# A written order of steps between the first feed-forward and the input projections, with the first half's norm and first operand listed earlier

## The chip, the cores and the metric

The kernel runs on one core of one Trainium2 chip. The metric is the device time in microseconds (us) of one execution; lower is better. Times are compared by the median of several executions. TensorE does the matrix products (PE in the profile, and PEld for its weight loads), VectorE is DVE, ScalarE is ACT, GpSimd is POOL, and SyncE (SP) issues most transfers.

## The reference, cut to what matters

One layer works on 512 new prompt tokens and 64 sample tokens (8 sequences of 8), 576 columns in all, with a model width of 1024.

```
h = modulate(rms_norm(x, n1_g), sh1, sc1)
x = x + 0.5 * g1 * swiglu(h, w1_gate, w1_up, w1_down)     # FF = 2816
h = modulate(rms_norm(x, nm_g), sh2, sc2)
z = h @ w_in                                              # 10240 columns: u v q k rv rg ga gb
...                                                       # gMLP, retention, merge, second FFN
```

The change lies between the second and the fourth of these lines: the last products with `w1_down`, the sum into `x`, the norm of the new `x`, its shift and scale, and the first products with `w_in`. `modulate(n, shift, scale)` is `n * (1 + scale) + shift`; the norm is `x * rsqrt(mean(x*x) + EPS)` over the 1024 channels of a token.

## The kernel before, in words

Channels lie on the partitions: `x` is one tile of 128 partitions x 8 chunks x 576 tokens, called `x_90` in the orders below and `x` in the profile. Every product is made from three fp32r products of a high and a low part (`hi` is a rounded copy, `lo` is the value less `hi`), so each operand and each weight needs a copy on ScalarE (`hi`, lines 564, 566, 667, 669) and a subtraction on VectorE (`lo`, lines 571, 575, 675, 679). The products with `w_in` are made by a Strassen-like scheme on halves of the tokens (two halves of 288) and halves of the channels: the blocks of the operand are called N11 (channels 0 to 511, tokens of half 0, negated), B21 (channels 512 to 1023, half 0), N1, B22 and so on. Each block is a tile of 4 chunks x 288 tokens, made in two pieces of two chunks.

Around the change the order of the work is written out by hand, as a string of step names (`INTO_MIX`). The function `run` (line 198) issues the steps in that order and then ties the instructions of each engine, SyncE excepted, into that order. So each engine works off its own part of the string, first in first out, and waits at its head. SyncE's queue holds only loads; each waits for its buffer to come free. The step names:

- `Dch`: a product of the last group of the first feed-forward, output chunk c, token part h (18 matmuls, line 485). The two parts are the columns 0 to 319 and 320 to 575, not the halves of 288.
- `rsch`: adds it into `x` (VectorE, line 466; for h = 1 also line 471 for the sample tokens), and `pxc`: adds the sample tokens' part on GpSimd (line 472).
- `sqch`: the square of half h of chunk c (ScalarE, line 428); `adch`: adds the squares up (GpSimd, line 433; the last of a half on VectorE). `spch`: stores that half to memory through ScalarE's queue (line 1223).
- `rdh`: one product with ones that sums over the channels (PE, line 444); `rqh`: the reciprocal root (ScalarE, line 448); `q0h q1h q2h`: its refinement (VectorE, lines 456, 459, 461; `q2h` also stores the row from GpSimd's queue, line 1231).
- `xph`: multiplies two chunks (pair p) of half h by the norm, in place (VectorE, line 533, waits until the stores of these chunks have read them); `bpc0`, `bpc`: scale and shift of one chunk (ScalarE, line 540); `sp` with one digit: the same for the sample tokens (VectorE, line 549).
- `N11hj`, `N11lj`, `B21hj`, `B21lj`, ...: high and low part of a piece of a block.
- `nhi nli whi wli`: high and low parts of the two weight tiles of projection i (i = 0, 1). `h0ai` is its product with N11 (24 matmuls, line 651), `sni` copies the two banks out (ScalarE, line 660), `h0bi` is the product with B21 into the same banks, after `sni` has read them.

In the string before, after the last chunk of token half 0 (`D70 rs70 sq70 ad70`), the second projection's weights (`nh1 nl1 wh1 wl1`) and the products `D31`, `D41` and `D51` are listed around `rd0 rq0 q00 q10 q20`, all four scalings `x00 x10 x20 x30` are listed with the operand's pieces, and four of them run back to back on VectorE.

Of the kernel before, what the change touches and what calls it, by code (L numbers as in the profile page):

```python
# [54 lines left out]
D00 D01 rs00 Wh2 sp00 sq00 ad00 Wl2 D10 rs01 px0 Wh3 sq01 ad01 Wl3 D11 sp01 rs10 sp10 sq10  # L55
ad10 Wh6 D20 rs11 Wl6 px1 sq11 sp11 ad11 D21 Wh4 rs20 sq20 Wl4 sp20 ad20 D30 rs21 Wh5 px2
sq21 Wl5 sp21 ad21 D40 rs30 sq30 sp30 ad30 Wh7 Wl7 D50 rs40 sq40 sp40 nh0 ad40 D60 rs50
sq50 nl0 sp50 ad50 wh0 D70 rs60 sq60 sp60 wl0 ad60 D31 rs70 sq70 nh1 sp70 ad70 nl1 D41 rs31
px3 sq31 sp31 rd0 wh1 D51 ad31 rq0 rs41 px4 q00 sq41 wl1 q10 sp41 ad41 q20 D61 rs51 px5 x00 sq51
sp51 ad51 D71 x10 b000 b010 x20 b100 x30 b110 N11h0 rs71 N11h1 rs61 px7 b210 N11l0 px6  # L60
sq71 N11l1 sq61 sp61 sp71 b300 ad61 h0a0 b310 b200 ad71 B21h3 B21h2 B21l3 B21l2 rd1 sn0 h0a1
rq1 q01 q11 q21 x01 h0b0 x11 b01 b00 s0 b11 s1 b10 tx0 sn1 tx1 N1h0 x21 h0b1 N1h1 N1l0 N1l1
b20 x31 b21 T2a1 b31 b30 h1a0 s3 e0s1 s2 B22h3 N3c1 B22h2 T2b1 N3h1 B22l2 p2bh T2h1 B22l3
h1a1 p2ah p2bl T2l1 e0s0 e0m0 p2al e0m1 N3l1 h1b0 p2S N4c1 p2U N4h1 T2a0 p2Sh P1 e1t0 T2b0
e1m0 p2Sl T2h0 h1b1 e1a0 T2l0 e1s0 P1s p2V N3c0 p2Uh P2 N4c0 N3h0 p2Ul N4h0 P5 e1a1 N3l0
# [1989 lines left out]
```

## Time and profile before

| | before |
|---|---|
| time, median of 3 runs | 1652.28 us (1651.71 to 1655.64) |
| time of the profiled execution | 1651.52 us |
| its span in the profile | 1649.7 us |
| granted TensorE clock, mean of the span | 0.996 |
| PE busy | 1618.0 us (98%), 12548 matmuls |
| DVE busy | 1152.9 us (70%) |
| ACT busy | 783.2 us (47%) |
| POOL busy | 292.0 us (18%) |

Times in the timeline count from the start of the span, so the profiled execution has 1.8 us outside it. In a timeline row stand the start, the time from the start of its first to the end of its last instruction, the engine, the line, what it writes from what it reads, how often, and in brackets the idle time before it with what ended that. A row of the table by stretches has the stretch, its length, then busy time and number of instructions of PE, PEld, DVE, ACT and POOL, the granted clock, and the transfers' share and rate.

### The profile page before, as it was taken

How to read it: one execution, taken by the hardware profiler on the slowest of the kernel's cores; microseconds unless marked ns; L12 is line 12 of the kernel's file. 1: busy time of each engine (PE TensorE's matmuls, PEld its weight loads, DVE VectorE, ACT ScalarE, POOL GpSimd, SP SyncE). 2: the span in 40 equal slices, each digit the busy share in tenths (PEclk: the TensorE clock that was granted, in tenths of full speed). 3: DMA queues.
4: the chain of work that ended last, by engine and by line, in shares of the span. 5: the costliest groups of instructions: out<-in, count | busy, mean ns of one | idle time of the engine just before them, and what ended most of it. 6: DMA issues, size and time to landing. Idle time of an engine off the chain costs nothing. (4 is left out here: it accounts for less than half of the span.)

```text
span 1649.7 us, 31367 instructions
## 1 busy us (share of the span) xinstructions
PE 1618.0 (98%) x12548; PEld 1554.7 (94%) x12548; DVE 1152.9 (70%) x1835; ACT 783.2 (47%) x1331; POOL 292.0 (18%) x372
## 2 busy tenths in 40 slices
PE   7999999999999999999999999999999999999997
PEld 4899999999999999999999999998999999999997
DVE  6867856676697777854788554676848868676773
ACT  5644524344564556553444454443236525343454
POOL 0000000000411111113346343454231000000002
PEclk9999999999999999999999999999999999999999
DMA  9553444332536776765467575799540333332331
GB/s 292 152 157 110 141 129 139 110 110 84 183 115 212 228 214 192 222 196 187 126 192 248 180 172 159 208 261 270 177 141 14 87 93 97 91 96 80 100 90 58
DMA packets 300212, 252.09 MB, mean 153 GB/s; under 512 B 13593, under 2 KB 260633, under 8 KB 300066
## 3 DMA queue, kind: packets, MB, share of 16 engines
q1 hardware_dynamic: 284594, 206.76, 41.5%
q0 software_dynamic: 13168, 40.97, 8.8%
q10 hardware_dynamic: 2304, 2.36, 0.4%
q8 instruction: 98, 1.61, 0.4%
q14 instruction: 48, 0.39, 0.1%
HBM read 207.01 MB, written 43.02 MB: 152 GB/s over the span
## 5 line engine op out<-in xcount | busy, mean ns | idle before, releaser
L651 PE MATMUL ps<-xa,whl 128*128 128x288 f32 x3000 | 420.6, 295 | 5.8 <-ACT xa L564 2.4
L651 PEld LDWEIGHTS ps<-xa,whl 128*128 128x128 f32 x3000 | 401.7, 189 | 18.5 <-issue 5.0
L651 PE MATMUL ps<-xs,whl 128*128 128x288 f32 x2040 | 287.2, 294 | 1.3 <-ACT sn L660 1.1
L651 PEld LDWEIGHTS ps<-xs,whl 128*128 128x128 f32 x2040 | 272.2, 188 | 11.6 <-ACT sn L660 4.6
L679 DVE TENSOR_TENSOR whl<-wraw,whl 128x1024 fp32r<-128x1024 f32 x192 | 234.5, 1223 | 54.0 <-ACT whl L669 45.1
L669 ACT CAST whl<-wraw 128x1024 fp32r<-128x1024 f32 x192 | 200.2, 1048 | 107.0 <-DVE wraw L793 67.3
L485 PEld LDWEIGHTS ps<-c,wd 128*128 128x128 f32 x1824 | 236.7, 188 | 3.5 <-issue 3.4
L485 PE MATMUL ps<-c,wd 128*128 128x320 f32 (+1 forms) x1824 | 239.9, 292 | 0.0
L485 PE MATMUL ps<-c,whl 128*128 128x256 f32 (+1 forms) x1368 | 186.9, 294 | 1.1 <-ACT c L195 0.7
L485 PEld LDWEIGHTS ps<-c,whl 128*128 128x128 f32 x1368 | 179.4, 188 | 3.4 <-ACT c L195 1.2
L472 POOL TENSOR_TENSOR x<-x,s 128x64 f32<-128x64 f32 x72 | 35.2, 489 | 796.9 <-DVE s L471 771.0
L466 DVE SCALAR_TENSOR_TENSOR x<-ps,gate,x 128x320 f32<-128x320 f32 (+1 forms) x128 | 61.1, 481 | 110.7 <-PE ps L485 110.7
L660 ACT COPY sn<-ps 128x288 f32<-128x288 f32 x195 | 77.2, 398 | 104.0 <-PE ps L651 103.7
L188 DVE TENSOR_TENSOR whl<-wraw,whl 128x1024 fp32r<-128x1024 f32 x56 | 76.3, 1364 | 66.7 <-ACT whl L187 66.1
L952 ACT CAST wd<-wraw 128x640 fp32r<-128x640 f32 (+2 forms) x58 | 45.4, 783 | 102.6 <-PE ps L485 95.5
L1353 PE MATMUL ps<-whl,xx 128*128 128x256 f32 x768 | 88.9, 276 | 0.0
L1353 PEld LDWEIGHTS ps<-whl,xx 128*128 128x128 f32 x768 | 88.0, 188 | 0.0
L651 PE MATMUL ps<-xs,whs 128*128 128x288 f32 x480 | 69.1, 292 | 0.0
L187 ACT CAST whl<-wraw 128x1024 fp32r<-128x1024 f32 x56 | 58.6, 1049 | 21.5 <-PE ps L485 13.3
L669 ACT CAST whs<-wraw 128x512 fp32r<-128x512 f32 x62 | 38.4, 620 | 55.7 <-PE ps L651 45.0
L651 PEld LDWEIGHTS ps<-xs,whs 128*128 128x128 f32 x480 | 64.8, 188 | 0.0
L957 DVE TENSOR_TENSOR wd<-wraw,wd 128x640 fp32r<-128x640 f32 (+2 forms) x58 | 53.5, 922 | 10.6 <-ACT wd L952 10.5
(285 smaller groups left out, 2219.0 us busy)
## 6 DMA issues: line engine op xcount, KB each, us to landing
ada<-in_w_ada_dram SPq DMA_DIRECT2D x56, 512.0 KB
wraw<-in_w_in_dram SPq DMA_DIRECT2D x96, 256.0 KB
wraw<-in_w_gate_dram SPq DMA_DIRECT2D x88, 256.0 KB
wraw<-in_w_up_dram SPq DMA_DIRECT2D x88, 256.0 KB
wraw<-in_w_in_dram SPq DMA_DIRECT2D x32, 512.0 KB
wraw<-in_w_down_dram SPq DMA_DIRECT2D x32, 384.0 KB
wraw<-in_w_down_dram SPq DMA_DIRECT2D x32, 320.0 KB
accd<-c POOLq DMA_DIRECT2D x32, 288.0 KB, 5.9
```

Source lines behind the costliest of these rows:

```text
L187: ACT.copy(out=hi, in_=raw)
L188: now["lo"] = (eng or DVE).tensor_tensor(out=lo, in0=raw, in1=hi.bitcast(F32), op=ALU.subtract)
L466: DVE.scalar_tensor_tensor(out=x[:, o:o + w], in0=ps[:, :w], scalar=g[:, c, 0:1], in1=x[:, o:o + w], op0=ALU.mult, op1=ALU.add)
L472: return lambda: POOL.tensor_tensor(out=x[:, NP:T], in0=x[:, NP:T], in1=u, op=ALU.add)
L485: PE.matmul(ps[:, :PW[h]], lhsT=s[:, k, c0:c0 + P], rhs=m[:, PART[h]], start=k == 0 and z == 0, stop=k == kc - 1 and z == 2,)
L651: PE.matmul(ps[:, :H], lhsT=s[:, j * P:(j + 1) * P], rhs=m[:, j, :], start=fresh and j == 0 and z == 0, stop=j == 3 and z == 2, skip_group ...
L660: ACT.copy(out=t, in_=ps[:, :H])
L669: ACT.copy(out=hl[:, 0], in_=src)
L679: now["lo"] = DVE.tensor_tensor(out=hl[:, 1], in0=src, in1=hl[:, 0].bitcast(F32), op=ALU.subtract)
L952: ACT.copy(out=hl[:, 0], in_=self.raw[c])
L957: DVE.tensor_tensor(out=lo, in0=self.raw[c], in1=hi.bitcast(F32), op=ALU.subtract)
L1353: PE.matmul(ps[:, :DV], lhsT=s, rhs=m, start=i == 0, stop=i == 23)
```

## The change

The change rewrites three lines of the string `INTO_MIX` and leaves all functions, sizes, buffers and step names as they are.

```diff
 sq21 Wl5 sp21 ad21 D40 rs30 sq30 sp30 ad30 Wh7 Wl7 D50 rs40 sq40 sp40 nh0 ad40 D60 rs50
-sq50 nl0 sp50 ad50 wh0 D70 rs60 sq60 sp60 wl0 ad60 D31 rs70 sq70 nh1 sp70 ad70 nl1 D41 rs31
-px3 sq31 sp31 rd0 wh1 D51 ad31 rq0 rs41 px4 q00 sq41 wl1 q10 sp41 ad41 q20 D61 rs51 px5 x00 sq51
-sp51 ad51 D71 x10 b000 b010 x20 b100 x30 b110 N11h0 rs71 N11h1 rs61 px7 b210 N11l0 px6
-sq71 N11l1 sq61 sp61 sp71 b300 ad61 h0a0 b310 b200 ad71 B21h3 B21h2 B21l3 B21l2 rd1 sn0 h0a1
-rq1 q01 q11 q21 x01 h0b0 x11 b01 b00 s0 b11 s1 b10 tx0 sn1 tx1 N1h0 x21 h0b1 N1h1 N1l0 N1l1
+sq50 nl0 sp50 ad50 wh0 D70 rs60 sq60 sp60 wl0 ad60 D31 rs70 sq70 sp70 ad70 nh1 rd0 rs31 D41
+px3 rq0 sq31 sp31 q00 wh1 ad31 q10 q20 rs41 px4 x00 sq41 sp41 ad41 D51 b000 x10 b010 rs51 px5
+N11h0 nl1 b100 b110 N11l0 D61 N11h1 sq51 sp51 rs61 px6 N11l1 ad51 sq61 sp61 D71 rs71 px7 ad61
+x20 sq71 sp71 h0a0 b200 b210 x30 B21h2 ad71 wl1 rd1 rq1 b300 b310 B21h3 q01 sn0 h0a1 q11 q21
+B21l2 B21l3 x01 h0b0 x11 b01 b00 s0 b11 s1 b10 tx0 sn1 tx1 N1h0 x21 h0b1 N1h1 N1l0 N1l1
```

On PE, `rd0` moves ahead of `D41` (it stood behind it), and `D71` moves behind `D61` as before; nothing else of PE's order changes. On VectorE the place from the last residual of half 0 to the operand's first low part reads, before (`ps_4871` is the bank of `rd0`, `h_4895` the norm, `whl_4840` and `whl_4873` the second projection's weights, `gate` the gate of the feed-forward):

```order
L675 SCALAR_TENSOR_TENSOR whl_4840<-wraw_4565,whl_4840 128x1024
L466 SCALAR_TENSOR_TENSOR x_90<-ps_4818,gate_1251,x_90 128x192
L456 SCALAR_TENSOR_TENSOR h_4901<-h_4895 128x288
L679 TENSOR_TENSOR whl_4873<-wraw_4568,whl_4873 128x1024
L459 SCALAR_TENSOR_TENSOR h_4901<-ps_4871,h_4901 128x288
L461 SCALAR_TENSOR_TENSOR h_4895<-h_4901,h_4895 128x288
L533 TENSOR_TENSOR x_90<-x_90,h_4895 128x2x288 x4
L571 SCALAR_TENSOR_TENSOR xa_4965<-x_90,xa_4965 128x2x288 x2
```

The same place of the changed kernel (`ps_4844`, `h_4869`, `whl_4842`, `whl_4876` and `xa_4917` are the same tiles under new numbers):

```order
L466 SCALAR_TENSOR_TENSOR x_90<-ps_4818,gate_1251,x_90 128x192
L456 SCALAR_TENSOR_TENSOR h_4874<-h_4869 128x288
L459 SCALAR_TENSOR_TENSOR h_4874<-ps_4844,h_4874 128x288
L461 SCALAR_TENSOR_TENSOR h_4869<-h_4874,h_4869 128x288
L533 TENSOR_TENSOR x_90<-x_90,h_4869 128x2x288 x2
L675 SCALAR_TENSOR_TENSOR whl_4842<-wraw_4565,whl_4842 128x1024
L571 SCALAR_TENSOR_TENSOR xa_4917<-x_90,xa_4917 128x2x288
L466 SCALAR_TENSOR_TENSOR x_90<-ps_4923,gate_1251,x_90 128x192
```

Some residual rows (lines 466 and 471) between these are not shown. Both splits of the second projection's weights left the stretch ahead of the scalings; two of the four scalings are now ahead of the first low part and two behind it.

On VectorE again, from the last sum of half 1 to its scaling (`all` holds the sums, `xa_5016` is B21), before:

```order
L571 SCALAR_TENSOR_TENSOR xa_4965<-x_90,xa_4965 128x2x288 x2
L433 TENSOR_TENSOR all_4587<-all_4587,h_4981 128x288
L575 TENSOR_TENSOR xa_5016<-x_90,xa_5016 128x2x288 x2
L456 SCALAR_TENSOR_TENSOR h_5055<-h_5053 128x288
L459 SCALAR_TENSOR_TENSOR h_5055<-ps_5021,h_5055 128x288
L461 SCALAR_TENSOR_TENSOR h_5053<-h_5055,h_5053 128x288
L533 TENSOR_TENSOR x_90<-x_90,h_5053 128x2x288 x2
```

and in the changed kernel (B21 is `xa_5012`, the norm of half 1 `h_5018`):

```order
L533 TENSOR_TENSOR x_90<-x_90,h_4869 128x2x288 x2
L433 TENSOR_TENSOR all_4587<-all_4587,h_4980 128x288
L679 TENSOR_TENSOR whl_4876<-wraw_4568,whl_4876 128x1024
L456 SCALAR_TENSOR_TENSOR h_5023<-h_5018 128x288
L459 SCALAR_TENSOR_TENSOR h_5023<-ps_5016,h_5023 128x288
L461 SCALAR_TENSOR_TENSOR h_5018<-h_5023,h_5018 128x288
L575 TENSOR_TENSOR xa_5012<-x_90,xa_5012 128x2x288 x2
L533 TENSOR_TENSOR x_90<-x_90,h_5018 128x2x288 x2
```

The two low parts of B21 moved from ahead of the refinement of half 1's norm to behind it, and the last weight split came in ahead of it.

On ScalarE, from the squares of half 1 to the first copies out of the banks (`h_4935`, `h_4978`, `h_4981` are squares, `ps_5021` is the bank of `rd1`), before:

```order
L428 ACTIVATE h_4935<-x_90 128x288
L1223 DMA x1d<-x_90 128x288
L540 ACTIVATE x_90<-x_90,mT,gain_4543 128x288 x4
L564 ACTIVATE xa_4965<-x_90 128x2x288 x2
L540 ACTIVATE x_90<-x_90,mT,gain_4543 128x288
L428 ACTIVATE h_4978<-x_90 128x288
L428 ACTIVATE h_4981<-x_90 128x288
L1223 DMA x1d<-x_90 128x288 x2
L540 ACTIVATE x_90<-x_90,mT,gain_4543 128x288 x3
L566 CAST xa_5016<-x_90 128x2x288 x2
L660 COPY sn_5023<-ps_4987 128x288
L660 COPY sn_5025<-ps_4988 128x288
```

and in the changed kernel:

```order
L564 ACTIVATE xa_4917<-x_90 128x2x288
L428 ACTIVATE h_4943<-x_90 128x288
L1223 DMA x1d<-x_90 128x288
L428 ACTIVATE h_4952<-x_90 128x288
L1223 DMA x1d<-x_90 128x288
L428 ACTIVATE h_4980<-x_90 128x288
L1223 DMA x1d<-x_90 128x288
L540 ACTIVATE x_90<-x_90,mT,gain_4543 128x288 x2
L566 CAST xa_5012<-x_90 128x2x288
L448 ACTIVATE h_5018<-ps_5016,epsT 128x288
L540 ACTIVATE x_90<-x_90,mT,gain_4543 128x288 x2
L566 CAST xa_5012<-x_90 128x2x288
```

The first operand's scalings and copies now stand ahead of the last three squares and their stores, and the reciprocal root of half 1 (line 448) stands between the two pieces of B21, ahead of the copies out of the banks.

## The prediction

> **What bounds the kernel now.** I read the page's first part, then busy time by stretches, then the timelines of the one stretch in which TensorE stands still. The page has TensorE almost full:
>
> ```profile
> PE 1618.0 (98%) x12548; PEld 1554.7 (94%) x12548; DVE 1152.9 (70%) x1835; ACT 783.2 (47%) x1331; POOL 292.0 (18%) x372
> ```
>
> So the change can save only where TensorE idles or runs slowly. The steps that it moves run from about 433 to 460 us. TensorE's timeline there (start, us from first start to last end, instruction, idle before) and two rows further on at full speed:
>
> ```profile
> 435.65 0.40 PE L444 MATMUL ps<-all,onesr 128*128 128x288 f32 x1
> 435.68 2.50 PE L485 MATMUL ps<-c,wd 128*128 128x256 f32 x18
> 438.02 4.41 PE L485 MATMUL ps<-c,xw 128*128 128x256 f32 x36
> 444.83 0.40 PE L651 MATMUL ps<-xa,whl 128*128 128x288 f32 x1 [2.40 <-ACT xa L564]
> 445.81 4.78 PE L651 MATMUL ps<-xa,whl 128*128 128x288 f32 x23 [0.58 <-DVE xa L571]
> 450.42 0.65 PE L444 MATMUL ps<-all,onesr 128*128 128x288 f32 x2
> ...
> 466.52 3.28 PE L651 MATMUL ps<-xs,whl 128*128 128x288 f32 x24
> 469.64 1.72 PE L651 MATMUL ps<-xa,whl 128*128 128x288 f32 x12
> ```
>
> The down-projection ends at 442.43; TensorE waits 2.40 us for the first high part of N11, then 0.58 us for its low part. The 24 matmuls of `h0a0` then end only at 450.42, though at full speed 24 matmuls hold TensorE for 3.12 us (466.52 to 469.64). The stretches tell why (PE, PEld, DVE, ACT, POOL busy, granted clock):
>
> ```profile
> 442.30:445.72 3.42, 0.53 (x3) 0.19 (x1) 3.42 (x8) 3.42 (x7) 2.13 (x3) 1.00 0.24 87
> 445.72:449.13 3.41, 3.32 (x14) 3.32 (x15) 1.33 (x4) 3.12 (x8) 1.15 (x2) 0.50 0.24 87
> 449.13:452.54 3.41, 3.41 (x26) 3.31 (x26) 2.25 (x4) 1.70 (x4) 0.00 (x0) 1.00 0.00 0
> ...
> 460.00:480.00 20.00, 20.00 (x156) 20.00 (x155) 18.99 (x32) 15.10 (x27) 1.46 (x3) 1.00 0.23 70
> ```
>
> Behind the almost idle 3.42 us stand 3.41 us at half clock: 14 matmuls instead of 26. From 442.43 to 450.42 are 7.99 us for 3.12 us of work: 4.87 us lost, 2.98 as waits and the other 1.9 to the half clock. That is all there is to win here. The last row shows the next limit: from 460 to 480 VectorE is busy 18.99 of 20 us.
>
> What ends the wait is a chain on VectorE and ScalarE, with its last links here:
>
> ```profile
> 437.63 0.46 DVE L456 SCALAR_TENSOR_TENSOR h<-h 128x288 f32<-128x288 f32 x1 [1.47 <-ACT h L448]
> 438.01 1.22 DVE L679 TENSOR_TENSOR whl<-wraw,whl 128x1024 fp32r<-128x1024 f32 x1
> 439.14 0.45 DVE L459 SCALAR_TENSOR_TENSOR h<-ps,h 128x288 f32<-128x288 f32 x1
> 439.63 0.58 DVE L461 SCALAR_TENSOR_TENSOR h<-h,h 128x288 f32<-128x288 f32 x1
> ...
> 440.59 3.58 DVE L533 TENSOR_TENSOR x<-x,h 128x576 f32<-128x576 f32 x4
> 444.10 0.41 DVE L466 SCALAR_TENSOR_TENSOR x<-ps,gate,x 128x192 f32<-128x192 f32 x1
> ...
> 445.01 1.54 DVE L571 SCALAR_TENSOR_TENSOR xa<-x,xa 128x576 fp32r<-128x576 f32 x2
> 447.25 0.46 DVE L433 TENSOR_TENSOR all<-all,h 128x288 f32<-128x288 f32 x1 [0.70 <-POOL all L433]
> 449.09 1.43 DVE L575 TENSOR_TENSOR xa<-x,xa 128x576 fp32r<-128x576 f32 x2 [1.39 <-ACT xa L566]
> 451.65 0.46 DVE L456 SCALAR_TENSOR_TENSOR h<-h 128x288 f32<-128x288 f32 x1 [1.12 <-ACT h L448]
> 452.14 0.46 DVE L459 SCALAR_TENSOR_TENSOR h<-ps,h 128x288 f32<-128x288 f32 x1
> 452.63 0.46 DVE L461 SCALAR_TENSOR_TENSOR h<-h,h 128x288 f32<-128x288 f32 x1
> 453.13 1.43 DVE L533 TENSOR_TENSOR x<-x,h 128x576 f32<-128x576 f32 x2
> ```
>
> ```profile
> 442.03 2.18 ACT L540 ACTIVATE x<-x,mT,gain 128x288 f32<-128x288 f32 x4
> 444.12 1.24 ACT L564 ACTIVATE xa<-x 128x576 fp32r<-128x576 f32 x2
> ...
> 453.92 1.97 ACT L540 ACTIVATE x<-x,mT,gain 128x224 f32<-128x224 f32 x4 [2.31 <-DVE x L533]
> 455.80 0.37 ACT L660 COPY sn<-ps 128x288 f32<-128x288 f32 x1
> ```
>
> **Part by part: the first wait.** `rd0` moves ahead of one product of 18 matmuls (438.02 less 435.68: 2.3 us), so it starts near 433.4. Before, 4.94 us pass from it to the first scaling (435.65 to 440.59), with the weight split of 1.22 us inside. Now nothing but the norm stands between: half 1, where that is so already, takes 1.23 us from its product (450.42) to the refinement and 1.48 us for the refinement's three (451.65 to 453.13). With two residual rows (0.5 us, as at 444.10) scaling starts near 436.6, 4 us earlier. ScalarE needs 3.4 us for four scalings and two copies (2.18 and 1.24) and issues a square and a store among them, so both high parts are there near 441.5, the second low part near 442.3. TensorE comes to N11 at 442.43 as before, and to its second piece after six matmuls, near 443.2. Both waits go, with 0.9 us to spare, and with them the half clock: **4.87 us**. If the chain is slower by more than 0.9 us, TensorE pays the excess.
>
> **The weight splits.** `nl1` (1.2 us) moves among the residuals, `wl1` behind half 1's last sum; VectorE does them while TensorE multiplies. They free the raw buffers, so SyncE's loads of the next projection come 5 to 7 us later. What covers that is this wait of SyncE's queue for its next free buffer:
>
> ```profile
> SPq L686 <- DVE wraw L802: 34.9, 1, 34.9
> ```
>
> After these loads it stood 34.9 us, so their lateness costs nothing unless a load takes tens of us. GpSimd's store of half 0's row also moves ahead, before two sums; its reader waits for half 1's row anyway.
>
> **What is late next: half 1's norm.** D71 ends at 442.4, its residual on VectorE near 443.1, GpSimd's part 443.5, the square near 444.0, the last sum (0.46 us) near 444.85. TensorE is through with `h0a0` at 445.55, so `rd1` starts without a wait, 0.7 us to spare. The rows above give 2.71 us from `rd1` (450.42) to the scaling (453.13): the refinement ends near 448.3. Behind it now stand B21's low parts, first one done near 449.0; TensorE wants it after `rd1` (0.27) and `h0a1` (3.12), near 449.1. That is a tie: between nothing and 0.6 us, and I take **0.1**.
>
> **Then the copies out of the banks.** Before, B21's low parts (1.43 us) stood ahead of this refinement; now they delay the scalings `x01 x11` to 449.6. ScalarE's four scalings start near 450.4 and take 1.97 us less an overlap of 0.1, the first bank is copied (0.37) near 452.7. TensorE wants to overwrite it (`h0b1`) near 452.2. A wait of 0.5 us that before does not have (there the copy ended at 456.2, TensorE came after 457); from a chain without any delay 0.3, with 0.2 us more on it 0.7. I take **0.5**.
>
> **Then VectorE itself.** It gains less than TensorE: 451.65 to about 446.7 is 4.9 us, less 1.43 for the low parts that moved behind, 3.5 us. Busy 18.99 of 20 us, it gives TensorE's weights out with little slack, and by 490 us TensorE's lead shrinks to VectorE's plus its slack of about 0.5: a further **0.4**, bounded by 0 and 0.8.
>
> **The sum.** 4.87 - 0.1 - 0.5 - 0.4 = 3.9 us against the profiled execution: 1651.52 - 3.9 = 1647.6. That run lies 0.76 us under the median of the runs shown, 1652.28. As I can't tell which the measurement resembles, I take **1648.0**, 4.3 us (0.26%) under the median. About 0.3%, or 5 us, is what a measurement of this kernel can tell from no change, so the forecast is an improvement just inside it: faster by more only below 1647.3.
>
> Whether a wait brings the half clock can be read at one more place, where 1.55 us of work in a stretch were enough to bring it:
>
> ```profile
> 1288.80:1292.22 3.42, 1.55 (x9) 1.33 (x10) 3.42 (x5) 3.42 (x4) 0.00 (x0) 1.00 0.00 0
> 1292.22:1295.64 3.42, 3.42 (x17) 3.42 (x16) 3.35 (x5) 0.44 (x2) 0.00 (x0) 0.50 0.81 233
> ```
>
> The two stretches lie 846.50 us apart, 248 times 3.413: a fixed grid. So how the idle time falls on it decides, and two stretches of 3.4 us, each with over 1.5 us idle, were followed by it.
>
> **Rivals.**
>
> *The half clock isn't these waits' doing* (chance 0.05). Then only the 2.98 us of waits go, less the three small terms: 1.9 us worse than forecast, 1649.9. Against it: both half-clock stretches follow directly on idle ones. The Trainium skill's page "TensorE: Matmul & The Clock Gate", section "HAM oscillation — how this bites in real kernels", states a rule of this kind: avoid gaps of over about 3.4 us. Gaps of 2.40 and 0.58 us would by it be harmless, and the trace doesn't agree.
>
> *The wait moves to `rd1`* (chance 0.17). Sums on GpSimd stretch beside VectorE's work:
>
> ```profile
> 436.24 0.81 POOL L433 TENSOR_TENSOR all<-all,h 128x288 f32<-128x288 f32 x1 [0.55 <-ACT h L428]
> 438.01 1.89 POOL L433 TENSOR_TENSOR all<-all,h 128x288 f32<-128x288 f32 x1 [0.68 <-ACT h L428]
> ```
>
> The last two steps of GpSimd ahead of `rd1` now run beside the scalings `x20 x30`. One sum stretched by 1.08, and the sample tokens' part by as much again, is 2.2 us, less 0.7 to spare: `rd1` waits up to 1.5 us, VectorE's lead shrinks alike, and if the grid falls badly part of the half clock is back: 1648.0 + 1.5 + 0.9 = 1650.4. For it speaks the row of 1.89, against it that GpSimd's other sum is at 0.81. The page "SBUF — State Buffer" of the Trainium skill, section "SBUF: two separate sides", states the mechanism: GpSimd shares a port pair with VectorE operations of two SBUF inputs, under an exclusive lock. The row of 1.89 beside VectorE's split of 1.22 agrees with it.
>
> *The grid shifts in our favour* (chance 0.14). With everything after 450 us earlier by 4 us, the idle time of 1288 to 1291 us falls on the grid anew and its half clock (1.7 us) goes as well: 1648.0 - 1.7 = 1646.3. Whether the grid stands alike in another execution the trace can't show.
>
> *ScalarE's stores block the chain, and it is slower* (chance 0.04). Three stores now stand directly ahead of B21 and of `rq1`. Each waits at its turn for an earlier transfer, and everything on ScalarE waits behind it. Before, such a wait stood once:
>
> ```profile
> L1223 ACTq DMA_DIRECT2D x1d<-x x16: 326/327/943, 411.8 to 446.3; - x16
> ...
>   ACT h L428: 2.1, 1
> ```
>
> If all three wait 2.1 us, ScalarE loses 6.3 us with almost nothing to spare; TensorE follows, the half clock (1.9) returns: 1648.0 + 6.3 + 1.9 = 1656.2. The sign turns from 4.3 us of such loss on. Against it: 15 of 16 stores held nobody up.
>
> *Nothing changes* (chance 0.02), 1652.3: the order is tied instruction by instruction, so only a first chain as long as before could do that.
>
> **How the numbers follow.** The forecast's own cases (0.58) run from 1646.5 to 1649.5, by the ends of the three small terms and the run's distance from the median. A quarter of them lies under 1647.3, 0.15, and with the grid's case faster is 0.29. Slower is the stores' case, 0.04; the rest, 0.67, is the same. For 8 in 10 the range takes in the grid's case with 0.7 us for the small terms at the lower end, 1645.6, and the `rd1` case with 0.5 us at the upper, 1650.9.
>
> **What would show it.** Right: TensorE's timeline has no wait between the last L485 row and the first L651 row near 442.4, clock 1.00 in the stretches there, a wait of about 0.5 us near 452 that ScalarE's copy (L660) ends, and the rows from 490 us on stand 3.9 us earlier. Wrong: a wait ahead of the L444 row of `rd1`, a 0.50 clock near 446, or a ScalarE wait for a store.

## The result, and the profile after

| | before | after |
|---|---|---|
| median, of 7 runs each on the same chip | 1651.71 us (1650.09 to 1655.64) | 1647.24 us (1645.43 to 1648.44) |
| profiled execution | 1651.52 us, span 1649.7 | 1648.44 us, span 1646.7 |

The ratio is 0.9972, with a 95% interval of 0.9963 to 0.9982: 4.47 us faster, where 4.3 were forecast. Against the 1652.28 us of the first three runs it is 5.04 us. The time itself is 0.8 us under the forecast 1648.0, mostly because the forecast started from those 1652.28 us and seven runs have a median 0.6 us lower. The two profiled executions lie 3.1 us apart, since that of after is the slowest of its seven.

The first part of the page of after shows the same work as before, TensorE 0.4 us less busy:

```profile
PE 1617.6 (98%) x12548; PEld 1554.9 (94%) x12548; DVE 1152.2 (70%) x1835; ACT 782.9 (48%) x1331; POOL 293.0 (18%) x372
```

TensorE's timeline of after, over the place where it stood still before and on to 490 us (L485 is the down-projection, L444 `rd0` and `rd1`, L651 the projections):

```profile
433.42 0.65 PE L444 MATMUL ps<-all,onesr 128*128 128x288 f32 x2
...
438.16 4.42 PE L485 MATMUL ps<-c,xw 128*128 128x256 f32 x36
442.41 3.29 PE L651 MATMUL ps<-xa,whl 128*128 128x288 f32 x24
445.93 0.72 PE L444 MATMUL ps<-all,onesr 128*128 128x288 f32 x2 [0.23 <-DVE all L433]
446.27 16.37 PE L651 MATMUL ps<-xa,whl 128*128 128x288 f32 x120
462.48 3.28 PE L651 MATMUL ps<-xs,whl 128*128 128x288 f32 x24
...
479.08 1.58 PE L651 MATMUL ps<-xa,whl 128*128 128x288 f32 x10 [0.31 <-DVE whl L679]
...
484.92 2.88 PE L651 MATMUL ps<-xa,whl 128*128 128x288 f32 x20 [0.50 <-DVE whl L679]
487.64 3.28 PE L651 MATMUL ps<-xs,whl 128*128 128x288 f32 x24
```

The down-projection's row ends at 442.58, 0.15 us later than before (442.43), but the 24 matmuls of `h0a0` follow at once, the first at 442.41, and in one piece. `rd1` starts at 445.93 instead of 450.42. The same stretches of after (busy time and instructions of PE, PEld, DVE, ACT, POOL, then the granted clock), and one from its start-up:

```profile
442.30:445.72 3.42, 3.40 (x27) 3.17 (x25) 2.58 (x7) 1.71 (x5) 2.89 (x3) 1.00 0.69 223
445.72:449.13 3.41, 3.20 (x23) 3.13 (x24) 3.04 (x6) 2.96 (x7) 0.16 (x1) 1.00 0.20 61
...
50.39:53.81 3.42, 3.42 (x16) 3.42 (x16) 2.31 (x7) 2.57 (x4) 0.00 (x0) 0.50 0.62 184
```

TensorE is busy 3.40 of the 3.42 us (0.53 before), and the stretch behind it has clock 1.00. The last row is a half-clock stretch at 50 us that the execution of before doesn't have, although the change moves nothing there; the one at 1292 us stands in after at 1289.43 still.

From the scaling to the first operand, and on to B21, on VectorE's timeline and then ScalarE's:

```profile
436.70 1.58 DVE L533 TENSOR_TENSOR x<-x,h 128x576 f32<-128x576 f32 x2
438.82 1.28 DVE L675 SCALAR_TENSOR_TENSOR whl<-wraw,whl 128x1024 fp32r<-128x1024 f32 x1
...
441.72 0.76 DVE L571 SCALAR_TENSOR_TENSOR xa<-x,xa 128x576 fp32r<-128x576 f32 x1 [0.36 <-ACT xa L564]
...
445.32 0.46 DVE L433 TENSOR_TENSOR all<-all,h 128x288 f32<-128x288 f32 x1 [0.70 <-POOL all L433]
445.70 1.22 DVE L679 TENSOR_TENSOR whl<-wraw,whl 128x1024 fp32r<-128x1024 f32 x1
447.22 0.46 DVE L456 SCALAR_TENSOR_TENSOR h<-h 128x288 f32<-128x288 f32 x1 [0.30 <-ACT h L448]
448.58 1.42 DVE L575 TENSOR_TENSOR xa<-x,xa 128x576 fp32r<-128x576 f32 x2
```

```profile
439.25 0.69 ACT L564 ACTIVATE xa<-x 128x576 fp32r<-128x576 f32 x1
441.00 0.69 ACT L564 ACTIVATE xa<-x 128x576 fp32r<-128x576 f32 x1
...
452.58 0.37 ACT L660 COPY sn<-ps 128x288 f32<-128x288 f32 x1
```

`rd0` is two matmuls. The first starts at 433.42, and before it started at 435.41:

```profile
435.41 0.65 PE L444 MATMUL ps<-all,onesr 128*128 128x288 f32 x2
```

So `rd0` comes 2.0 us earlier; scaling starts at 436.70 (440.59 before). The first weight split (438.82) stands behind two scalings, the second (445.70) behind the last sum. The high parts are there at 439.94 and 441.69, the second low part at 442.48. GpSimd's last two sums ahead of `rd1`, with the sample tokens' part `px7` between them:

```profile
442.10 1.05 POOL L433 TENSOR_TENSOR all<-all,h 128x288 f32<-128x288 f32 x1 [0.33 <-ACT h L428]
443.24 0.76 POOL L472 TENSOR_TENSOR x<-x,s 128x64 f32<-128x64 f32 x1
443.97 1.32 POOL L433 TENSOR_TENSOR all<-all,h 128x288 f32<-128x288 f32 x1
```

The second sum ends at 445.29. VectorE, which had stood idle for 0.70 us until then, ends the last sum at 445.78, and `rd1` has waited 0.23 us for it.

### The profile page after: what moved, and what is told of

Its sections match the earlier page's. It is cut to its first block, busy times and chain, and to the rows that moved or that the text cites. A ratio compares the mean times of both kernels' runs of the same rounds, so it can differ in the third digit from the quotient of the medians.

```text
span 1646.7 us, 31365 instructions
## 1 busy us (share of the span) xinstructions
PE 1617.6 (98%) x12548; PEld 1554.9 (94%) x12548; DVE 1152.2 (70%) x1835; ACT 782.9 (48%) x1331; POOL 293.0 (18%) x372
## 4 chain that ended last, share of the span: by engine, by line
PE 81%; DVE 8%; DMA 5%; ACT 3%; issue 2%; POOL 1%; SPq 0%; POOLq 0%; ACTq 0%; DVEq 0%
PE ps L651 36%; PE ps L485 29%; PE ps L1353 5%; PE ps L1583 3%; PE ps L307 2%; DVE whl L679 1%; DMA wraw<-in_w_down_dram 1%; ACT whl L669 1%; PE ps L1483 1%; DMA wraw<-in_w_a_dram 1%; DMA xa<-in_w_ada_dram 1%; PE ps L1445 1%; PE ps L1366 1%; PE ps L1489 1%; DVE xa L575 0%
## 5 line engine op out<-in xcount | busy, mean ns | idle before, releaser
L651 PE MATMUL ps<-xa,whl 128*128 128x288 f32 x3000 | 420.7, 295 | 3.5 <-DVE whl L679 1.6
L651 PEld LDWEIGHTS ps<-xa,whl 128*128 128x128 f32 x3000 | 401.7, 189 | 16.3 <-issue 3.4
L651 PE MATMUL ps<-xs,whl 128*128 128x288 f32 x2040 | 287.0, 294 | 1.3 <-ACT sn L660 1.3
L651 PEld LDWEIGHTS ps<-xs,whl 128*128 128x128 f32 x2040 | 272.0, 188 | 11.6 <-issue 5.0
L485 PEld LDWEIGHTS ps<-c,wd 128*128 128x128 f32 x1824 | 236.7, 188 | 3.5 <-issue 3.4
L485 PE MATMUL ps<-c,wd 128*128 128x320 f32 (+1 forms) x1824 | 239.8, 292 | 0.0
L485 PE MATMUL ps<-c,whl 128*128 128x256 f32 (+1 forms) x1368 | 186.9, 294 | 1.1 <-ACT c L195 0.7
L485 PEld LDWEIGHTS ps<-c,whl 128*128 128x128 f32 x1368 | 179.5, 188 | 3.3 <-ACT c L195 0.9
L651 PE MATMUL ps<-xs,whs 128*128 128x288 f32 x480 | 69.1, 292 | 0.0
L651 PEld LDWEIGHTS ps<-xs,whs 128*128 128x128 f32 x480 | 64.8, 188 | 0.0
```

The lines of the kernel that those rows point to most:

```text
L485: PE.matmul(ps[:, :PW[h]], lhsT=s[:, k, c0:c0 + P], rhs=m[:, PART[h]], start=k == 0 and z == 0, stop=k == kc - 1 and z == 2,)
L651: PE.matmul(ps[:, :H], lhsT=s[:, j * P:(j + 1) * P], rhs=m[:, j, :], start=fresh and j == 0 and z == 0, stop=j == 3 and z == 2, skip_group ...
```

## The experiments

**The theory.** TensorE's two waits at N11 and the half clock that they bring are what went; the rearrangement removes them only as a whole, because `rd0`, the weight splits and the scalings delay the same chain one behind another; and part of the gain is given back by the copy ahead of `h0b1`, then by VectorE. **The rivals.** One part alone does it (`rd0`, the splits or the scalings); or the half clock is no consequence of the waits; or what limits the gain is the copy, and VectorE has slack.

Beside the medians the tables and texts use the *local gain*: by how much an execution gains on that of before between the matmul that starts at 429 us there and the one that starts at 502 us, counted at the same matmul of both traces. It leaves out what two executions differ by elsewhere; by itself it is one execution's number, but one kernel that was profiled twice (the 17 matmuls below) gave 1.19 and 1.15 us. For after it is 3.48 us. The experiments ran on three chips; each ratio is to the kernel before on the same chip.

### One part undone, one part alone

**`rd0` back** behind the product, in the changed kernel:

```diff
-... ad70 nh1 rd0 rs31 D41
-px3 rq0 ...
+... ad70 nh1 rs31 D41
+px3 rd0 rq0 ...
```

> The changed kernel, but with rd0 behind D41 again, one product of 18 matmuls later. If the gain comes from the whole chain from rd0 to N11 standing earlier, this puts the chain back by 2.2 us where it has 0.9 us to spare: waits of about 1 to 1.5 us in all at the first products with N11, no half clock there (the idle time of a stretch stays under 1.5 us), and a time 1 to 2 us above the changed kernel, about 1648.5 to 1649. If the place of rd0 does not matter because the weight splits and the scalings held the chain, no wait there and the time of the changed kernel, 1647.2.

Measured: 1649.73 us, ratio to before 0.9985 (0.9977 to 0.9994); local gain 1.56, 1.9 us less than after. TensorE's timeline:

```profile
441.98 1.19 PE L651 MATMUL ps<-xa,whl 128*128 128x288 f32 x6 [0.33 <-DVE xa L571]
443.56 2.50 PE L651 MATMUL ps<-xa,whl 128*128 128x288 f32 x17 [0.40 <-DVE xa L571]
446.88 0.72 PE L444 MATMUL ps<-all,onesr 128*128 128x288 f32 x2 [0.82 <-DVE all L433]
```

The product that `rd0` now waits behind is 2.0 us long (the one ahead of it goes from 431.38 to 433.42 in after). 1.9 us of that come back at TensorE, most of it in the three small waits of 1.55 us together (0.23 in after), without a half clock. Of the parts that were undone one at a time `rd0` costs most (`wl1`, and both splits together, were not put back), but nearly half of the gain stays without it.

**The splits late, alone**: in the kernel before, only `nl1` goes behind `N11h0` and `wl1` behind `B21h2`.

```diff
-sq50 ... nh1 sp70 ad70 nl1 D41 rs31
+sq50 ... nh1 sp70 ad70 D41 rs31
-... sq41 wl1 q10 ... N11h0 rs71 ... B21h3 B21h2 B21l3 ...
+... sq41 q10 ... N11h0 nl1 rs71 ... B21h3 B21h2 wl1 B21l3 ...
```

> The kernel before, with only the two splits of the second projection's weights moved: nl1 behind N11h0, wl1 behind B21h2. If the splits alone held the chain (1.2 us of VectorE each, one ahead of the norm and one inside it), the 2.98 us of waits and the half clock go, and the time is that of the changed kernel, about 1647.5. If all parts count, about 1.5 to 2.5 us of wait stay, because rd0 still stands behind D41 and the four scalings still run back to back; whether the half clock stays then hangs on the grid: 1649 to 1651.5.

Measured: 1649.58 us, 0.9987 (0.9979 to 0.9995); local gain 1.59. TensorE's timeline and its stretches:

```profile
443.90 0.40 PE L651 MATMUL ps<-xa,whl 128*128 128x288 f32 x1 [0.43 <-ACT xa L564]
446.03 4.70 PE L651 MATMUL ps<-xa,whl 128*128 128x288 f32 x23 [1.72 <-DVE xa L571]
```

```profile
442.36:445.78 3.42, 1.51 (x11) 1.09 (x9) 3.42 (x7) 3.02 (x6) 1.00 (x3) 1.00 0.03 8
445.78:449.19 3.41, 3.16 (x13) 3.16 (x14) 2.58 (x4) 2.59 (x6) 1.65 (x2) 0.50 0.74 232
```

The first wait falls from 2.40 to 0.43 us, the second grows from 0.58 to 1.72, since the moved split now stands between the two pieces. Together they still leave TensorE 1.9 us idle in one stretch, and the half clock is there again. What the splits are worth here is 0.89 us, the gain that stands at `rd1` and up to 483 us. The other 0.70 us of the local gain come between 483 and 491 us, where the order on VectorE and ScalarE differs from before though the diff names none of these instructions: the split of one `whs` (line 679), for instance, starts at 488.81 behind two of `whl` and stood ahead of them before. So this second part, and its share of the time, can't be put down to the place of the two splits alone.

**The scalings late, alone**: in the kernel before, `x20 x30` and their steps go behind N11.

```diff
-... D71 x10 b000 b010 x20 b100 x30 b110 N11h0 rs71 N11h1 rs61 px7 b210 N11l0 px6
-sq71 N11l1 sq61 sp61 sp71 b300 ad61 h0a0 ...
+... D71 x10 b000 b010 N11h0 b100 b110 N11l0 N11h1 rs71 rs61 px7 N11l1 px6 x20
+sq71 sq61 sp61 sp71 x30 b210 b300 ad61 h0a0 ...
```

> The kernel before, with only the scalings of the third and fourth pair (x20, x30) and their scale-and-shift steps moved behind N11. If the four scalings back to back (3.58 us) held N11, the wait falls by their half, 1.3 us or more, and with it the half clock: about 1648 to 1649. If N11 was held by what stands ahead of the first scaling, the wait falls by 0.5 to 1 us only, B21 comes later in its turn and takes that back: 1650 to 1652.5, no change.

Measured: 1652.65 us, 1.0003 (0.9994 to 1.0012), no change; local gain -0.51. TensorE's timeline:

```profile
442.86 0.40 PE L651 MATMUL ps<-xa,whl 128*128 128x288 f32 x1 [1.51 <-ACT xa L564]
443.65 1.36 PE L651 MATMUL ps<-xa,whl 128*128 128x288 f32 x6 [0.39 <-DVE xa L571]
445.41 2.50 PE L651 MATMUL ps<-xa,whl 128*128 128x288 f32 x17 [0.40 <-DVE xa L571]
...
455.86 4.30 PE L651 MATMUL ps<-xa,whl 128*128 128x288 f32 x31 [0.90 <-ACT sn L660]
```

The waits at N11 are 2.3 us instead of 2.98 and no half clock follows, so 1.4 us are won up to `rd1`: it starts at 447.94 instead of 450.42, and 1.1 us of that this execution was ahead already. By 483 us they are lost and 0.5 us more: 1.3 us up to 462, where TensorE waits 0.90 us for the copies, and the rest beyond, with a wait of 0.33 us for weights at 481.6. Here removing a wait at the front is worth nothing, since the chain behind it isn't shortened as well.

### Whether the half clock is these waits' doing

**Work in the wait**: in the kernel before, 17 matmuls whose result is never read (they write a bank that is overwritten afterwards) stand ahead of the first product with N11 (`fill[0]` is an operand tile of the last down-projection).

```diff
+        def h0a(self):
+            self.A = [bank() for _ in range(2)]
+            if self.n == 0:
+                wh, x = self.w["n11"][0], fill[0]
+                for _ in range(17):
+                    PE.matmul(
+                        self.A[1][:, :H], lhsT=wh[:, 0:P], rhs=x[:, 0:H], start=True, stop=True, skip_group_check=True
+                    )
+            for ps, w in zip(self.A, ("n11", "n21")):
+                prod(ps, self.w[w], op("N11"), True)
```

> The kernel before, with 17 matmuls of 288 columns ahead of the first product with N11 that nobody reads (they go to a bank that the next product overwrites): TensorE works 2.2 us of its 2.40 us of wait and starts the product at the same time as before. If the half clock near 446 us comes from the idle time, the stretch stays at clock 1.00 and rd1 starts 1.5 to 1.9 us earlier than in the kernel before, while the waits for N11's parts end at the same times as there: median about 1.2 us lower, as the half clock need not come in every execution. If the half clock has another cause it stays, and the time is that of the kernel before or a little above.

Measured: 1652.52 us, 1.0003 (0.9993 to 1.0013). By the time, nothing changed; by the trace, much did. TensorE's timeline near 441 us and near 754 us:

```profile
440.65 2.42 PE L879 MATMUL ps<-c,whl 128*128 128x288 f32 x17
443.21 0.40 PE L651 MATMUL ps<-xa,whl 128*128 128x288 f32 x1
444.20 3.30 PE L651 MATMUL ps<-xa,whl 128*128 128x288 f32 x23 [0.59 <-DVE xa L571]
447.34 0.65 PE L444 MATMUL ps<-all,onesr 128*128 128x288 f32 x2
...
753.69 1.16 PE L1397 MATMUL ps<-c,c 128*128 128x128 f32 x8 [2.46 <-POOL c L1345]
```

The operand comes no earlier, but TensorE is busy while it waits. No half clock follows, the 23 matmuls take 3.30 instead of 4.78 us, and from the end of the down-projection (440.81) to `rd1` 6.53 us pass instead of 7.99: 1.5 us less with 17 matmuls more, and a local gain of 1.19 us. So the idling brought the half clock here. This gain is kept up to 751 us and lost there: TensorE waits 2.46 us (1.13 in the execution of before) and runs at half clock behind that. The stretch:

```profile
755.41:758.82 3.41, 3.41 (x18) 3.41 (x17) 2.08 (x6) 1.56 (x3) 2.37 (x3) 0.50 0.52 161
```

What was late is a load: VectorE waits for the table of rotations. The load was issued at 737.65, so 7.4 us pass from its issue to VectorE's first use; in the execution of before it is 6.1 (740.77 to 746.88).

```profile
745.09 0.75 DVE L1341 TENSOR_TENSOR c<-c,rope 64x576 f32<-64x576 f32 x1 [6.32 <-DMA rope<-in_rope_dram]
```

Whether this loss at 751 us belongs to the 17 matmuls or to one execution, two more runs asked.

**The same kernel again**, without any edit:

> The kernel with the 17 unread matmuls in TensorE's wait once more, since its trace had clock 1.00 there and yet its median was not lower. If what took the gain back near 751 us (a wait of 2.46 us instead of 1.13, and a half clock behind it) was chance, this profile has a wait of about 1.2 us there, and TensorE keeps about 1.2 us of gain to the end; the median is then 0.5 to 1.2 us below the kernel before. If it belongs to the added matmuls, the wait near 751 us is again over 2 us and the median again about 1652.5.

Measured: 1651.92 us, 1.0002 (0.9994 to 1.0011), local gain 1.15; near 446 us the clock is 1.00 again, the wait for the rotations is 6.27 us, TensorE's wait 2.39 us, and the half clock stands at 756.04.

**The same 17 matmuls in the changed kernel**, by the same edit:

> The changed kernel with the same 17 unread matmuls ahead of the first product with N11, where it has no wait to fill. Their own work is 2.2 us of TensorE, of which the waits behind them (0.23 us at rd1, 0.4 us near 452 us, 0.3 us near 478 us) take up to 0.9 us back: 1.3 to 2.2 us above the changed kernel, 1648.5 to 1649.4, if adding matmuls costs only their work. If added matmuls have another price of about 2 us that sits elsewhere in the program, 1650.5 to 1651.5, and then the earlier fill's flat median says nothing against the half clock's part.

Measured: 1650.91 us, 0.9993 (0.9983 to 1.0002); local gain 1.66.

The matmuls lower the local gain from 3.48 to 1.66 us, a little less than their own 2.2 (17 at the 0.13 us of 3.12 us for 24), and again 2.9 us are lost near 751 us, with a wait of 2.47 us and a half clock at 754.60. In the three profiles with the added matmuls VectorE stands idle for 6.27 to 6.32 us at that place, in the other nine for 4.98 to 5.46 (seven of the nine name the load of another constant, `hc`, as the one that came last). Four of this kernel's eleven runs took 1648.3 to 1649.3 us, about what its own work alone was to cost, so the price elsewhere need not come in every execution. The flat median of the kernel of before with the matmuls is thus the sum of a local gain and a price elsewhere, and it doesn't speak against the half clock being the waits' doing. Why the load lands 1.3 us later when TensorE has 17 more instructions 300 us before was not settled.

### What limits the gain

**The copies earlier**: the changed kernel, with the copies out of the banks (`sn1`) ahead of the scale and shift of `b01`.

```diff
-B21l2 B21l3 x01 h0b0 x11 b01 b00 s0 b11 s1 b10 tx0 sn1 tx1 ...
+B21l2 B21l3 x01 h0b0 x11 sn1 b01 b00 s0 b11 s1 b10 tx0 tx1 ...
```

> The changed kernel, with the copies of the second projection's banks (sn1) ahead of ScalarE's four scalings of half 1 instead of behind them. If VectorE is the bound behind this place, the wait near 452.5 us goes (0.4 us) but TensorE waits as much more for VectorE's weight split near 478 us, and from 490 us on nothing is gained: time 1647.2 as the changed kernel, within 0.5 us. If that wait itself was what cost, TensorE stands 0.4 us earlier from 490 us on.

Measured: 1647.93 us, 0.9973 (0.9964 to 0.9982): the time of after. By 462 us the gain is 4.38 us instead of after's 4.09, so the wait at `h0b1` has gone; by 502 us it is 3.50, against 3.48. TensorE's timeline shows where it went:

```profile
478.22 1.57 PE L651 MATMUL ps<-xa,whl 128*128 128x288 f32 x10 [0.43 <-DVE whl L679]
```

TensorE comes to the next weights earlier and waits for VectorE longer. VectorE, not the copy, sets what is left of the gain. The other profiles fit this at one instruction of VectorE that no experiment moves, its first of line 789, here in the executions of before and of after:

```profile
468.02 0.68 DVE L789 TENSOR_TENSOR wraw<-wraw,wraw 128x512 f32<-128x512 f32 x1
```

```profile
464.80 0.69 DVE L789 TENSOR_TENSOR wraw<-wraw,wraw 128x512 f32<-128x512 f32 x1
```

Counted from the same matmul at 429 us as the local gain, it comes 3.27 us earlier in after and as much here, 1.33 with `rd0` back, 0.98 in the kernel of before with the 17 matmuls, and 0.72 later with the scalings late. In nine of the eleven profiles the local gain is 0.20 to 0.24 us more than this lead. The two others are the splits late and the next run, in which the order of instructions changed farther on.

**A low part earlier too**: the same kernel with `B21l2` ahead of `q01`.

```diff
-... B21h3 q01 sn0 h0a1 q11 q21
-B21l2 B21l3 x01 ...
+... B21h3 B21l2 q01 sn0 h0a1 q11 q21
+B21l3 x01 ...
```

> The same, and B21's first low part ahead of the refinement of half 1's norm, where VectorE stands idle for 0.3 us. If VectorE is the bound, its rows from 449 us on come 0.3 us earlier and TensorE gains 0.3 us from 490 us on against the changed kernel, 3.7 to 3.8 us against the kernel before instead of 3.5; the time is 1646.9, which the runs can hardly tell. If B21's low part or the norm is what TensorE waits for, it loses 0.4 us instead.

Measured: 1648.05 us, 0.9976 (0.9965 to 0.9986); local gain 3.61. VectorE comes 0.28 us earlier at line 789 than in the run above, as expected, but TensorE gains 0.1 us, not 0.3: it waits 0.22 us for a copy of ScalarE (line 660) at 474 us, which the others don't. That copy stands behind a weight's copy (line 669) here and ahead of it in the run above, though the diff names neither. In time the run can't be told from after or from the run above it. So it doesn't price the tie at B21's low part cleanly.

**A split back**: the changed kernel with `nl1` directly ahead of `rd0`.

```diff
-... ad70 nh1 rd0 ... N11h0 nl1 b100 ...
+... ad70 nh1 nl1 rd0 ... N11h0 b100 ...
```

> The changed kernel, with only the weight split nl1 (1.2 us of VectorE) back ahead of the first half's norm. If the chain from rd0 to N11 has 0.9 us to spare or less, up to 0.5 us of waits come back at N11, and the later chain to rd1 is late as well: TensorE 0.5 to 1.3 us later than in the changed kernel from 490 us on, time 1647.7 to 1648.5. If the split is hidden where it was, no difference.

Measured: 1648.76 us, 0.9984 (0.9975 to 0.9993); local gain 2.14, 1.34 less than after. TensorE's timeline:

```profile
442.93 2.48 PE L651 MATMUL ps<-xa,whl 128*128 128x288 f32 x17 [0.39 <-DVE xa L571]
446.25 0.72 PE L444 MATMUL ps<-all,onesr 128*128 128x288 f32 x2 [0.85 <-DVE all L433]
```

A split of 1.28 us on VectorE costs TensorE 1.34 us. At N11 after has 0.8 us to spare (the second low part is there at 442.48, and TensorE comes to it with the eighth of the 24 matmuls at 443.32), so only a wait of 0.39 us comes back there. The chain to `rd1`, which waits 0.23 us in after already, has nothing to spare and pays the rest.

**The scalings back**: the changed kernel with `x20 x30` directly behind `x10`.

```diff
-... D51 b000 x10 b010 ... x20 sq71 sp71 h0a0 b200 b210 x30 B21h2 ...
+... D51 x10 x20 x30 b000 b010 ... sq71 sp71 h0a0 b200 b210 B21h2 ...
```

> The changed kernel, with the four scalings of half 0 back to back again, x20 and x30 ahead of N11's steps. If only the start of the chain counted (rd0 and the weight splits), this costs nothing at N11 and frees GpSimd's sums later: 1647.0 to 1647.5. If the scalings' place counts too, N11's low part and rd1 come 0.5 to 1.2 us later: 1648 to 1648.8.

Measured: 1647.83 us, 0.9976 (0.9965 to 0.9986); local gain 3.01, 0.47 less than after. The time lies between the two ranges expected and can't be told from after's. TensorE's timeline, then GpSimd's:

```profile
442.00 3.89 PE L651 MATMUL ps<-xa,whl 128*128 128x288 f32 x24
445.99 0.72 PE L444 MATMUL ps<-all,onesr 128*128 128x288 f32 x2
```

```profile
443.50 0.80 POOL L433 TENSOR_TENSOR all<-all,h 128x288 f32<-128x288 f32 x1
444.26 0.32 POOL L472 TENSOR_TENSOR x<-x,s 128x64 f32<-128x64 f32 x1
444.54 0.82 POOL L433 TENSOR_TENSOR all<-all,h 128x288 f32<-128x288 f32 x1
```

The 24 matmuls take 0.6 us longer, since the low parts come later behind four scalings. VectorE is idle here from 443.82 to 445.39, and GpSimd's two sums take 0.80 and 0.82 us and `px7` 0.32, where in after they took 1.05, 1.32 and 0.76; `rd1` starts 0.1 us behind the last matmul. So in after it is VectorE's work beside them that stretches them: the scalings `x20 x30` (443.08 to 444.62) for `px7` and the second sum, the second low part (441.72 to 442.48) for the first sum. The two traces agree with the Trainium skill's page "SBUF — State Buffer", section "SBUF: two separate sides": a GpSimd operation and a VectorE operation with two SBUF inputs exclude each other from a port pair.

Put side by side: out of the whole, the return of `rd0` costs 1.9 us, that of `nl1` 1.3 and that of the scalings 0.5; alone in the kernel before, the splits are worth 0.9 us at their place, and the late scalings lose 0.5. So the parts lean on each other, but that they work only as a whole says too much: no half clock comes back at this place when one part is undone.

## Why the prediction was right, step by step

One more row of before, from TensorE's timeline, to compare with 487.64 of after:

```profile
491.07 3.28 PE L651 MATMUL ps<-xs,whl 128*128 128x288 f32 x24
```

Both executions leave the down-projection at nearly the same time (442.43 and 442.58), so the starts of the same matmul can be subtracted:

| term of the sum | forecast | measured in the two traces |
|---|---|---|
| waits at N11 and half clock, up to `rd1` | 4.87, with `rd1` on time | 450.42 - 445.93 = 4.49: `rd1` waits 0.23, and the down-projection ends 0.15 later |
| tie at B21 and copies ahead of `h0b1` | -0.1 - 0.5 | (466.52 - 462.48) - 4.49 = -0.45 |
| VectorE up to 490 us | -0.4 | (491.07 - 487.64) - 4.04 = -0.61 |
| sum | 3.9 | 3.43 |

- **The first wait.** As forecast. Scaling was to start near 436.6 and started at 436.70; the second low part was to be there near 442.3 and was there at 442.48. TensorE didn't wait. The start of `rd0` came out right, 433.4, in part by luck: the forecast took 435.65 for its start before, which is the start of its second matmul (the first is at 435.41), and 2.3 us for the product that it passes, which has 0.3 us of `rd0` itself in it (each of the two products ahead of it takes 2.04 us from start to start). The two slips cancel. The return of one split (1.34 us for 1.28) and that of `rd0` (1.9 for 2.0) show that both belong to the step.
- **The half clock.** It was right that it follows the idle stretch. With work in the place of idling it went, though the operand came no earlier; with 1.9 us of idling left in one stretch it stayed. The rival that these waits have nothing to do with it falls.
- **`rd1`.** The forecast gave it 0.7 us to spare; it waited 0.23 us. The step that was off is the time of GpSimd's work ahead of it, which the forecast took unstretched and the rival of the wait that moves to `rd1` had named: `px7` took 0.76 us instead of 0.32 and the second sum 1.32 instead of 0.81, together 0.95 us more, which is the 0.7 to spare and the wait. (The first sum stretched by 0.24 too, but ended before `px7` could start.) The rival had 2.2 us of stretch and up to 1.5 of wait. It had the mechanism; in size the forecast was nearer.
- **The tie and the copies.** 0.45 us, for the 0.6 forecast. B21's first low part, half of the 1.42 us from 448.58 on, was there at 449.3 (forecast 449.0), and no wait shows ahead of its product; the copy was done at 452.95, a quarter of a microsecond later than forecast. The wait forecast near 452 us has no row of its own in after; it is inside the row that starts at 446.27, whose 120 matmuls take 16.37 us and took 15.99 before. Moving the copy earlier gives back 0.3 us at once.
- **VectorE.** 0.61 us for the 0.4 forecast, and within its bounds. That it is a bound and no mere wait was shown by the earlier copies: 0.3 us more by 462 us, nothing more by 502; the lead of VectorE at line 789 says the same.
- **ScalarE's stores.** This rival falls. Line 1223 of after, from the view of its stores:

```profile
L1223 ACTq DMA_DIRECT2D x1d<-x x16: 326/326/412, 411.8 to 444.0; - x16
...
  ACT h L428: 2.1, 1
```

  One store still holds up one square for 2.1 us, as before; the three at B21 hold up nobody.

- **The loads of the next projection.** SyncE's wait that was to cover their lateness shrank from 34.9 to 24.1 us, and it is still long:

```profile
SPq L686 <- DVE wraw L802: 24.1, 1, 24.1
```

- **The grid.** It was thought that the half clock at 1292 us might go too. In the profile of after it is there, at 1289.43; in four of the ten experiments' profiles, those of the scalings late, the scalings back, and two of the three with added matmuls, it is not. The kernel of before with the matmuls has it in one of its two profiles (1291.31) and not in the other. So it comes and goes with the execution.
- **The total.** The local sum is 3.43 us, 0.4 below the forecast's 3.9, and the forecast added 0.4 for the distance between the profiled run and the median. The medians differ by 4.47 us. About 1 us of that is thus not found in the two profiled executions, which differ by 3.1 us. It is of the size by which executions scatter: the seven runs of after with granted clocks of 0.998, 0.997 and 0.996 took 1645.43, 1646.45 to 1648.17, and 1648.44 us. One half-clock stretch more or less is 0.001 of that clock (half of 3.41 in 1647 us), and the profiled run is the one at 0.996. Which part of that 1 us the change brought stays open. The forecast's mechanism is shown; that the difference of the medians came within 0.2 us of it is in part luck.

## What to carry to other kernels

When a bounding engine waits for a chain, look at every instruction that stands between its links on every engine: here three parts moved together, the dearest of them undone left nearly half of the gain, and one of them alone was worth nothing because the next waits took it back. Count a gain at the same instruction of both traces, place by place, before the medians are read: a flat median hid a gain of 1.2 us here and a loss of 2.9 us 300 us later. Compare the order of the instructions on every engine too, well behind the edit: two of these edits changed it where they touched nothing. And an idle time costs more than its length where the clock follows it, so waits that fall into different stretches can be cheaper than the same sum in one: 2.30 us brought no half clock with the scalings late, 2.15 us did with the splits late.

## What the runs showed of the hardware

**How much idling brings the half clock.** From the matmul records of the twelve profiles, each laid on its own grid of 3.413 us, TensorE's idle time of every stretch from 440 us to the end was added up. 25 of the 26 stretches that were followed by half clock had 1.69 us or more of idle time, one had 1.59; of the others, up to the last half clock at the very end, none had more than 1.60. So it turns near half of the stretch, and the idle time may lie in several pieces. In the start-up, from 46 to 50 us, this doesn't hold: idle times of about 1.96 us brought it there in two executions, and 1.88 to 1.96 us in four others did not. The Trainium skill's page "TensorE: Matmul & The Clock Gate", section "HAM oscillation — how this bites in real kernels", has the rule of no gaps over about 3.4 us; the single wait of 1.59 us of the kernel with the earlier copies, at 751.84 us and with a half clock at 753.27, is under half of that, and was enough here.

**A price far away.** 17 matmuls more on TensorE came with a load that landed 1.3 us later, 300 us on, in all three profiles of the two kernels that have them; the cause is open.
